# One tuned encoder kernel: the root of six of its eight RMS norms reaches the partitions by other ways

## The chip, the cores and the metric

The kernel runs on one core of a Trainium2 chip. The metric is the device time of one execution in microseconds (us). The core has a matrix engine (TensorE, PE in the rows; its weight loads are PEld), a vector engine (VectorE, DVE), a scalar engine (ScalarE, ACT), a general engine (GpSimd, POOL) and a queue of transfers that one more engine issues in order (SyncE, SP). Each engine takes its own instructions in program order and waits on semaphores for the others.

## The reference, cut to what matters

One layer of a hybrid encoder, applied to 1024 prompt tokens and 256 sample tokens with 1024 features, all in float32, then a last norm:

```python
def rmsnorm(x, w):
    xf = x.astype(jnp.float32)
    y = xf * lax.rsqrt(jnp.mean(xf * xf, -1, keepdims=True) + EPS)
    return (y * w.astype(jnp.float32)).astype(x.dtype)
```

The layer has three sublayers with residual adds. Each begins with this norm. The first is a mixing block (a gated DeltaNet, which is a chunked linear recurrence, beside a gated two-layer branch, gMLP), then cross-attention into 256 + 256 memory tokens, which are normalised too, then a SwiGLU feed-forward block. So a norm is needed of the tokens before the mixing block, before the attention, of the memory, before the feed-forward block, and at the end. For one token the sum of squares runs over the 1024 features, and its inverse root then scales all 1024 features of the token.

## The kernel before

**Tiling.** Activations lie feature-major: 1024 features are 8 tiles (KT = 8) of 128 partitions, and the tokens run along the free axis. There are three token blocks: 0 and 1 of 512 prompt tokens each, 2 of 256 sample tokens. Large products are float32 split in two rounded parts (hi and lo, or whi and wlo for weights), and three matmuls stand for one product. They come from helper lines L108 (`mm`), so L108 is nearly every matmul of the trace. `split` makes the parts: ACT writes hi (L125), DVE or POOL subtracts to get lo (L126).

**What sets the order.** The program is built by Python generators. PE's order is written out: the main stream of products runs, and side generators (a norm is one) `yield` a number of nanoseconds of PE work after which their next step is put in. `lag`, `lag2` and `pace` are such numbers. So a norm's products stand at a fixed place in PE's stream, ready or not. The other engines' instructions are ordered by a scheduler that sees dependencies and its own costs. SP's transfers are issued in its order, one behind another.

**A norm.** `Norm.add` squares tile after tile on ACT (L259) and sums them on DVE (L260) into `nacc`. `Norm.rest` sums over the partitions with narrow products into a bank, so that each token's sum lies on a partition; L280 makes the mean, and L231 to L235 on DVE find the inverse root by three Newton steps into the tile `nst`, 128 partitions x 4 (token number c * 128 + p on partition p, column c), or x 2 for block 2. The root must then come from "token on a partition" to "token on the free axis, the same in all partitions". Before, that is one float32 product for each 128 tokens: the column of roots, broadcast, as weights against the identity (`cst`), into a PSUM bank. In the trace they are the rows `bank<-cst,nst`: four products for 512 tokens, two for 256, and each product leaves two records. Then L298 on DVE scales each of the 8 tiles by weight and root (`nt<-mem,sm,bank` for the memory, `x<-x,sm,bank` for the others), and a sink passes it on: stores of the memory tiles (`md`), `split` of the feed-forward input, stores of the output (`yT`).

```python
pb = bank()
for c in range(nb):
    mm(pb[:, c * P : (c + 1) * P], y[:, c : c + 1].to_broadcast([P, P]), ident)
```

**The places.** Eight norms use this code. Two (the mixing block's) are not touched. The memory's norm runs around 90 to 105 us, while the in-projection of block 2 goes through PE; on DVE and ACT the gMLP's gelu groups run then (L497 to L500, the `gt` and `vg` tiles), then the layer norm's statistics (L519 to L525, `sums`), the DeltaNet's decay rates (L549 to L568, `ab`, `beta`, `wk`, `gm`), and the scaling of the gMLP's `vg` (L529). PE takes `gm` in the product `bank<-cst,gm` and `vg` in `bank<-sw,vg`. The feed-forward norms of blocks 0, 1, 2 stand at 1295, 1337 and 1355 us, in the attention's out-projection (`OutProj.run`; L1491 is its residual add out of PSUM) and the first products behind it. The final norms of blocks 1 and 0 are at 2093 and 2127 us (`last_norm`). There the sample block's feed-forward inputs (`graw`, L2333) are loaded by SP, split into `gs` (L126), and the down-projection's results are added by L2254.

## Time and profile before

Three runs took 2184.56, 2186.04 and 2183.62 us, median 2184.56. The profile is of one more execution.

| | us |
|---|---|
| median of the runs | 2184.56 |
| profiled execution, its own time | 2183.43 |
| profiled execution, first to last instruction (span) | 2181.6 |
| PE busy | 2168.0 (99 %) |
| DVE busy | 1356.4 (62 %) |
| ACT busy | 885.9 (41 %) |
| POOL busy | 592.4 (27 %) |
| mean granted clock of TensorE | 0.999 of full speed |

In a row of the timeline stand the start in us, the duration in us (of all the instructions that the row groups, with their count behind the x), engine, line, operation, output and inputs by tile name, shapes; in brackets the idle time of the engine ahead of it and who ended it. Matmuls overlap in the pipeline, so a matmul's price is the distance between the starts of two neighbours, not its duration.

### The profile page before, as it was taken

How to read it: one execution, taken by the hardware profiler on the slowest of the kernel's cores; microseconds unless marked ns; L12 is line 12 of the kernel's file. 1: busy time of each engine (PE TensorE's matmuls, PEld its weight loads, DVE VectorE, ACT ScalarE, POOL GpSimd, SP SyncE). 2: the span in 40 equal slices, each digit the busy share in tenths (PEclk: the TensorE clock that was granted, in tenths of full speed). 3: DMA queues.
4: the chain of work that ended last, by engine and by line, in shares of the span. 5: the costliest groups of instructions: out<-in, count | busy, mean ns of one | idle time of the engine just before them, and what ended most of it. 6: DMA issues, size and time to landing. Idle time of an engine off the chain costs nothing.

```text
span 2181.6 us, 31947 instructions
## 1 busy us (share of the span) xinstructions
PE 2168.0 (99%) x12184; PEld 1888.0 (87%) x12184; DVE 1356.4 (62%) x2615; ACT 885.9 (41%) x1651; POOL 592.4 (27%) x399
## 2 busy tenths in 40 slices
PE   9999999999999999999999999999999999999998
PEld 8988888888988888888988888888888888888888
DVE  7867688786874846677644556544434444478575
ACT  6533363544535553125544523332322323343454
POOL 2010100101001010052412432566666665200031
PEclk9999999999999999999999999999999999999999
DMA  5221323323244546631522421322222222493531
GB/s 195 92 93 57 109 63 96 82 66 95 75 122 121 171 133 228 204 128 58 175 73 111 156 97 64 104 87 83 83 78 81 83 97 91 149 347 119 205 112 59
DMA packets 194296, 253.04 MB, mean 116 GB/s; under 512 B 76932, under 2 KB 109268, under 8 KB 194142
## 3 DMA queue, kind: packets, MB, share of 16 engines
q1 hardware_dynamic: 177886, 227.14, 31.6%
q10 hardware_dynamic: 16256, 23.86, 3.0%
q8 instruction: 95, 1.56, 0.3%
q14 instruction: 59, 0.48, 0.1%
HBM read 178.02 MB, written 72.94 MB: 115 GB/s over the span
## 4 chain that ended last, share of the span: by engine, by line
PE 95%; DVE 2%; ACT 1%; DMA 1%; issue 0%; SPq 0%; POOL 0%; DVEq 0%; ACTq 0%; POOLq 0%
PE bank L108 94%; PE bank L121 1%; DMA braw<-gq 1%; DVE gb L832 0%; PE bank L398 0%; DVE aT L827 0%; DVE nt L298 0%; DVE nacc L260 0%; DMA uc<-usd 0%; DVE sw L1014 0%; POOL lo L126 0%; DVE wlo L126 0%; ACT junk L524 0%; ACT whi L125 0%; DVE bhl L126 0%
## 5 line engine op out<-in xcount | busy, mean ns | idle before, releaser
L108 PE MATMUL bank<-hi,whi 128*128 128x512 f32 (+1 forms) x1976 | 700.6, 355 | 0.0
L108 PE MATMUL bank<-lo,whi 128*128 128x512 f32 (+1 forms) x1976 | 687.0, 348 | 0.0
L108 PE MATMUL bank<-hi,wlo 128*128 128x512 f32 (+1 forms) x1976 | 686.6, 347 | 0.0
L108 PEld LDWEIGHTS bank<-hi,wlo 128*128 128x128 f32 x1976 | 373.6, 189 | 47.8
L108 PEld LDWEIGHTS bank<-hi,whi 128*128 128x128 f32 x1976 | 374.4, 189 | 45.1 <-issue 1.1
L108 PEld LDWEIGHTS bank<-lo,whi 128*128 128x128 f32 x1976 | 374.5, 190 | 43.3 <-issue 0.2
L126 POOL TENSOR_TENSOR wlo<-raw,whi 128x1024 fp32r<-128x1024 f32 x65 | 158.1, 2433 | 296.5 <-ACT whi L125 296.5
L125 ACT ACTIVATE whi<-raw 128x1024 fp32r<-128x1024 f32 (+1 forms) x136 | 137.0, 1009 | 249.1 <-PE bank L108 216.8
L126 DVE TENSOR_TENSOR wlo<-raw,whi 128x1024 fp32r<-128x1024 f32 (+1 forms) x71 | 80.8, 1141 | 74.7 <-ACT whi L125 74.4
L108 PE MATMUL bank<-bhl,whi 128*128 128x512 f32 x408 | 125.8, 390 | 0.0
L126 POOL TENSOR_TENSOR wlo<-x,whi 128x1024 fp32r<-128x1024 f32 x40 | 96.6, 2414 | 47.5 <-ACT whi L125 47.5
L2136 DVE TENSOR_TENSOR x<-x,bank 128x512 f32<-128x512 f32 x21 | 14.5, 689 | 124.4 <-ACT x L1931 124.4
L108 PEld LDWEIGHTS bank<-bhl,whi 128*128 128x128 f32 x408 | 76.5, 188 | 16.1
L710 DVE SCALAR_TENSOR_TENSOR acc<-craw,sm,acc 128x510 f32<-128x510 f32 (+1 forms) x96 | 73.2, 763 | 23.8 <-ACT acc L708 22.1
L1944 DVE SCALAR_TENSOR_TENSOR t<-t,x 128x512 f32<-128x512 f32 x42 | 63.9, 1521 | 28.7 <-ACT t L1943 28.7
L125 ACT ACTIVATE whi<-x 128x1024 fp32r<-128x1024 f32 (+1 forms) x48 | 49.2, 1025 | 77.5 <-PE bank L108 69.6
L108 PE MATMUL bank<-bhl,wlo 128*128 128x512 f32 x204 | 79.6, 390 | 0.2 <-DVE wlo L126 0.2
L1953 DVE SCALAR_TENSOR_TENSOR t<-bank,t 128x512 f32<-128x512 f32 (+1 forms) x44 | 24.5, 558 | 81.4 <-PE bank L108 81.4
L108 PE MATMUL bank<-bhl,ahl 128*128 128x512 f32 x312 | 75.0, 395 | 0.0
L1082 ACT ACTIVATE gs<-bank 128x512 f32<-128x512 f32 (+1 forms) x60 | 31.2, 520 | 101.2 <-PE bank L108 93.9
L1931 ACT ACTIVATE x<-bank 128x512 f32<-128x512 f32 x63 | 37.6, 597 | 82.0 <-PE bank L108 79.3
L108 PEld LDWEIGHTS bank<-bhl,ahl 128*128 128x128 f32 x312 | 58.7, 188 | 13.6
(420 smaller groups left out, 4462.6 us busy)
## 6 DMA issues: line engine op xcount, KB each, us to landing
raw<-in_w_gu SPq DMA_DIRECT2D x44, 512.0 KB, 3.3
braw<-gq SPq DMA_DIRECT2D x14, 1024.0 KB, 6.9
raw<-in_w_g SPq DMA_DIRECT2D x20, 512.0 KB, 3.3
gq<-t SPq DMA_DIRECT2D x33, 256.0 KB, 2.0
gtd<-gs ACTq DMA_DIRECT2D x32, 256.0 KB, 2.1
w<-in_w_dn SPq DMA_DIRECT2D x8, 1024.0 KB, 9.6
raw<-in_w_qkv SPq DMA_DIRECT2D x12, 512.0 KB, 3.4
gq<-r SPq DMA_DIRECT2D x22, 256.0 KB, 2.0
```

Of the source, the lines that this page charges most:

```text
L108: self.nc.tensor.matmul(out, l, r, start=start, stop=stop, skip_group_check=more)
L121: self.nc.tensor.transpose(out, x, ident)
L125: self.last_hi = self.nc.scalar.activation(hi, src, AF.Copy).ins
L126: (eng or self.nc.vector).tensor_tensor(out=lo, in0=src, in1=f32(hi), op=ALU.subtract)
L710: V.scalar_tensor_tensor(out=dst, in0=src, scalar=wj, in1=dst, op0=ALU.mult, op1=ALU.add)
L1082: S.activation(t, ps, AF.Tanh, scale=0.5)
L1931: S.activation(t, ps, AF.Copy)
L1944: V.scalar_tensor_tensor(out=t, in0=t, scalar=1.0, in1=src, op0=ALU.add, op1=ALU.mult)
L1953: V.scalar_tensor_tensor(out=out, in0=u, scalar=sign, in1=t, op0=ALU.mult, op1=ALU.mult)
L2136: V.tensor_tensor(out=c22, in0=c22, in1=pe, op=ALU.add)
```

## The change

The sums, the roots, the weights' scaling and the sinks stay. Three ways now bring the root to the partitions:

- The memory norm and the feed-forward norm of block 0 take the way over DRAM: SP writes `nst` (4 numbers, 16 bytes a partition) to `rows_d`, and SP reads the 512 numbers back into all 128 partitions of the norm's own accumulator `nacc`. No product is made. The scaling (L323 now) reads its root from SBUF, not from a bank, through a view that puts the token order right (`quad`).
- The feed-forward norms of blocks 1 and 2 and the final norms of blocks 1 and 0 are "spread": DVE rounds the root to its high part (L294, `nhi`), subtracts for the low part (L295), and multiplies the identity by each part, broadcast (L299, tile `nd`, 128x512 or 128x256; L293 rounds a column of ones). Then two products of the ones with `nd` as moving operand, as wide as the block and with rounded inputs, fill the bank. `nd` takes buffers of the tag `nsq`, from which the squares and, at the end, the `graw` tiles come too.
- The two norms of the mixing block are unchanged, as is the norm of block 2 at the end.

`lag2` grows from 2800 to 6500 for the memory (and ROW = 3500 ahead of it), and from 2800 to 7000 for block 0; for the others the place of the products stays (SPREAD is taken out of `lag2` and put back).

```diff
@@ -260,7 +260,7 @@
                 (eng or V).tensor_tensor(out=self.acc, in0=self.acc, in1=sq, op=ALU.add)
             self.k += 1
 
-        def rest(self, xk, wcol, sink, pace=1300, shared=(), lag=1500, ks=range(KT), inplace=False, ready=None, halves=1, lag2=2800, rooms=(), behind=None):
+        def rest(self, xk, wcol, sink, pace=1300, shared=(), lag=1500, ks=range(KT), inplace=False, ready=None, halves=1, lag2=2800, rooms=(), behind=None, row=None, spread=False):
 
             p, n = self.p, self.n
             nb = n // P
@@ -272,30 +272,55 @@
             for c in range(nb):
                 for t in parts:
                     mm(pc[:, c : c + 1], t[:, c * P : (c + 1) * P], one, t is parts[0], t is parts[-1])
-            y = p.tile([P, 4 if p is xp else 16], F32, tag="nst", name="nst", bufs=2)[:, :nb]
+            rest_ = p.tile([P, 4 if p is xp else 16], F32, tag="nst", name="nst", bufs=2)
+            y = rest_[:, :nb]
             ms, sc = pc[:, 4 : 4 + nb], pc[:, 8 : 8 + nb]
             with ExitStack() as st:
                 if behind is not None:
                     st.enter_context(tc.issue_after(behind()))
                 V.tensor_scalar(out=ms, in0=pc[:, :nb], scalar1=1.0 / D, scalar2=EPS, op0=ALU.mult, op1=ALU.add)
             K.root_end = rsqrt(y, ms, sc)
-            yield lag2
-            pb = bank()
-            for c in range(nb):
-                mm(pb[:, c * P : (c + 1) * P], y[:, c : c + 1].to_broadcast([P, P]), ident)
+            if row is not None:
+                SY.dma_start(row.rearrange("(p c) -> p c", c=nb), y)
+                yield ROW
+                SY.dma_start(self.acc, row.unsqueeze(0).to_broadcast([P, n]))
+                yield lag2
+                rb = pb = self.acc.rearrange("q (p c) -> q c p", c=nb)
+            elif spread:
+                yield lag2 - SPREAD
+                rounded = p.tile([P, 16], F32R, tag="nhi", name="nhi")
+                yhi, ylo = f32(rounded[:, 4 : 4 + nb]), rest_[:, 8 : 8 + nb]
+                V.tensor_copy(rounded[:, 0:1], one)
+                V.tensor_copy(rounded[:, 4 : 4 + nb], y)
+                V.tensor_tensor(out=ylo, in0=y, in1=yhi, op=ALU.subtract)
+                spreads = []
+                for part in (yhi, ylo):
+                    t = p.tile([P, 512], F32R, tag="nsq", name="nd", bufs=self.sq)[:, :n]
+                    V.tensor_tensor(out=quad(t), in0=ident.unsqueeze(1).to_broadcast([P, nb, P]), in1=part.unsqueeze(2).to_broadcast([P, nb, P]), op=ALU.mult)
+                    spreads.append(t)
+                yield SPREAD
+                pb = bank()[:, :n]
+                for t in spreads:
+                    mm(pb, rounded[:, 0:1].to_broadcast([P, P]), t, t is spreads[0], t is spreads[-1])
+            else:
+                yield lag2
+                pb = bank()[:, :n]
+                for c in range(nb):
+                    mm(pb[:, c * P : (c + 1) * P], y[:, c : c + 1].to_broadcast([P, P]), ident)
             while ready is not None and not ready():
                 yield 300
-            if shared:
+            like = (lambda x: x) if row is None else quad
+            if shared and row is None:
                 rb = self.acc
-                S.activation(rb, pb[:, :n], AF.Copy)
+                S.activation(rb, pb, AF.Copy)
             for k in ks:
                 if k in shared:
                     S.activation(xk(k), xk(k), AF.Copy, scale=sm[:, wcol + k : wcol + k + 1])
-                    G.tensor_tensor(out=xk(k), in0=xk(k), in1=rb, op=ALU.mult)
+                    G.tensor_tensor(out=like(xk(k)), in0=like(xk(k)), in1=rb, op=ALU.mult)
                     sink(k, xk(k))
                     continue
                 t = bank() if k in rooms else xk(k) if shared or inplace else p.tile([P, 512], F32, tag="nsq", name="nt", bufs=self.sq)[:, :n]
-                V.scalar_tensor_tensor(out=t, in0=xk(k), scalar=sm[:, wcol + k : wcol + k + 1], in1=pb[:, :n], op0=ALU.mult, op1=ALU.mult)
+                V.scalar_tensor_tensor(out=like(t), in0=like(xk(k)), scalar=sm[:, wcol + k : wcol + k + 1], in1=pb, op0=ALU.mult, op1=ALU.mult)
                 sink(k, t)
                 yield pace * n / 512
 
@@ -313,12 +338,12 @@
         rsqrt(y, ms, sc)
         yield lag2
 
-    def norm(p, xk, n, wcol, sink, pace=1300, step=700, lag=1500):
+    def norm(p, xk, n, wcol, sink, pace=1300, step=700, lag=1500, **more):
         nm = Norm(p, n)
         for k in range(KT):
             nm.add(xk(k))
             yield step
-        yield from nm.rest(xk, wcol, sink, pace, lag=lag)
+        yield from nm.rest(xk, wcol, sink, pace, lag=lag, **more)
 
     def to_h(h, b, mine=(1, 3, 5, 7)):
         return lambda k, t: split(h[b][0][:, k, :], h[b][1][:, k, :], t, V if k in mine else G)
@@ -460,6 +485,7 @@
     begin.close()
 
     done = set()
+    rows_d = dp.tile([2, 512], F32, name="rows_d")
 
     def other_norms():
         nm = Norm(xp, 512)
@@ -472,7 +498,7 @@
         done.add(1)
         mem = x_load(a["memT"], 0, 512, "mem")
         yield 6000
-        yield from norm(xp, lambda k: mem[:, k, :], 512, S_MEM, lambda k, t: SY.dma_start(md[k], t))
+        yield from norm(xp, lambda k: mem[:, k, :], 512, S_MEM, lambda k, t: SY.dma_start(md[k], t), lag2=6500, row=rows_d[0])
 
     norms = K.side(other_norms())
 
@@ -1523,7 +1549,7 @@
                 if sinks is None:
                     norm_b = nms[b].rest(xk, wcol, to_h(hs, b), 600)
                 else:
-                    norm_b = nms[b].rest(xk, wcol, sinks(b, hs), PACES[b], ks=range(KT) if b != 1 else SECOND_KS, inplace=True, lag2=LAGS2[b])
+                    norm_b = nms[b].rest(xk, wcol, sinks(b, hs), PACES[b], ks=range(KT) if b != 1 else SECOND_KS, inplace=True, lag2=LAGS2[b], row=rows_d[1] if b == 0 else None, spread=b > 0)
                 K.pending[id(hs), b] = K.side(norm_b)
             self.x = x
 
@@ -2293,7 +2319,7 @@
             (SY if k % 2 else S).dma_start(a["yT"][:, k, t0 : t0 + n], t)
 
         if b < 2:
-            K.side(nm.rest(lambda k: x2[b][:, k, :], S_FIN, sink, PACEF, SHARED[b], LAGF[b], lag2=LAGF2[b]))
+            K.side(nm.rest(lambda k: x2[b][:, k, :], S_FIN, sink, PACEF, SHARED[b], LAGF[b], lag2=LAGF2[b], spread=True))
             return
         pb = bank()
         ms, y = pb[:, :n], pb[:, n : 2 * n]
@@ -2418,9 +2444,10 @@
 MIX = 6500
 A1, A2, A3, A4 = 1200, 800, 2000, 600
 DEC, CONV = 1200, 600
-FIRST_W, PACES, LAGS2 = 9000, (600, 1300, 600), (2800, 9500, 9500)
+FIRST_W, PACES, LAGS2 = 9000, (600, 1300, 600), (7000, 9500, 9500)
 LAGX = (26000, 17000, 9000)
 FIRST_V = (1, 3, 5, 6, 7)
+ROW, SPREAD = 3500, 2500
 LAG0, LAGF, LAGF2, PACEF = 9700, (8000, 6000, 1500), (9000, 9000, 2800), 1000
 
 SHARED, EARLY_K = ((1, 4, 6), (1, 3, 5, 7)), (1, 3)
```

PE's order is the same but for these products: 4 fewer at the memory, 4 fewer at block 0, two in place of four at blocks 1 (feed-forward and final) and 0 (final), two in place of two at block 2. On the other engines rows move. Lines behind L280 are renumbered (L298 is L323 now, L1491 is L1517, L519 is L545, L555 to L568 are L581 to L594).

VectorE at the memory norm, before: the last four of eight scalings `nt` and what follows.

```order
L298 SCALAR_TENSOR_TENSOR nt<-mem,sm,bank 128x512
L500 SCALAR_TENSOR_TENSOR vg,sums<-gt,bank 128x248
L621 COPY ab<-bank 128x16
L298 SCALAR_TENSOR_TENSOR nt<-mem,sm,bank 128x512 x2
L498 SCALAR_TENSOR_TENSOR gt<-gt,bank 128x248
L298 SCALAR_TENSOR_TENSOR nt<-mem,sm,bank 128x512
L500 SCALAR_TENSOR_TENSOR vg,sums<-gt,bank 128x248
L621 COPY ab<-bank 128x16
L519 TENSOR_TENSOR sums<-sums 128x4
L550 TENSOR_TENSOR wk_1280<-ab,rows 128x80
```

The same place now, from a little further on; between L545 (L519 before) and these rows stand one more L323 and the four L575 (L549):

```order
L576 TENSOR_TENSOR wk_1263<-ab,rows 128x80
L546 TENSOR_SCALAR sums<-sums 128x4
L323 SCALAR_TENSOR_TENSOR nt<-mem,sm,nacc 128x512
L577 SCALAR_TENSOR_TENSOR wk_1263<-wk_1263 128x80
L547 TENSOR_SCALAR sums<-sums 128x4
L323 SCALAR_TENSOR_TENSOR nt<-mem,sm,nacc 128x512
L589 TENSOR_SCALAR wk_1263<-wk_1263 128x80
L581 TENSOR_SCALAR wk_1263<-wk_1263 128x80
L582 RECIPROCAL wk_1263<-wk_1263 128x80
L323 SCALAR_TENSOR_TENSOR nt<-mem,sm,nacc 128x512
L583 TENSOR_TENSOR wk_1263<-wk_1263 128x80
```

Before, all eight scalings stood ahead of L519 (`sums`). Now the first stands behind two more gelu groups, and four of the eight stand behind L545, between the small instructions on `wk` that make `gm`.

VectorE at the feed-forward norm of block 1, from the end of the root (L235) to the first scaling. Before:

```order
L235 SCALAR_TENSOR_TENSOR nst<-bank,nst 128x4
L1491 SCALAR_TENSOR_TENSOR x_12386<-bank,x_12386 128x256
L260 TENSOR_TENSOR nacc<-nacc,nsq 128x256
L1491 SCALAR_TENSOR_TENSOR x_12386<-bank,x_12386 128x256
L260 TENSOR_TENSOR nacc<-nacc,nsq 128x256
L1491 SCALAR_TENSOR_TENSOR x_12386<-bank,x_12386 128x256
L260 TENSOR_TENSOR nacc<-nacc,nsq 128x256
L298 SCALAR_TENSOR_TENSOR x_12385<-x_12385,sm,bank 128x512 x2
```

Now:

```order
L235 SCALAR_TENSOR_TENSOR nst<-bank,nst 128x4
L294 CAST nhi<-nst 128x4
L295 TENSOR_TENSOR nst<-nst,nhi 128x4
L1517 SCALAR_TENSOR_TENSOR x_12384<-bank,x_12384 128x256
L260 TENSOR_TENSOR nacc<-nacc,nsq 128x256
L1517 SCALAR_TENSOR_TENSOR x_12384<-bank,x_12384 128x256
L299 TENSOR_TENSOR nd<-cst,nhi 128x512
L260 TENSOR_TENSOR nacc<-nacc,nsq 128x256
L299 TENSOR_TENSOR nd<-cst,nst 128x512
L1517 SCALAR_TENSOR_TENSOR x_12384<-bank,x_12384 128x256
L260 TENSOR_TENSOR nacc<-nacc,nsq 128x256
L323 SCALAR_TENSOR_TENSOR x_12383<-x_12383,sm,bank 128x512 x2
```

L294, L295 and the two L299 have come in; the second L299 stands behind two more sums L260, whose places relative to L1517 have changed by one.

VectorE at the feed-forward norm of block 2, before:

```order
L1896 TENSOR_TENSOR x_12384<-x_12384,x_12385 128x1024
L235 SCALAR_TENSOR_TENSOR nst<-bank,nst 128x2
L1953 SCALAR_TENSOR_TENSOR t<-bank,t 128x512
L126 TENSOR_TENSOR lo_12699<-x_12384,hi_12698 128x1024
L298 SCALAR_TENSOR_TENSOR x_12386<-x_12386,sm,bank 128x256 x4
L126 TENSOR_TENSOR lo_12701<-x_12386,hi_12700 128x256
```

Now:

```order
L1922 TENSOR_TENSOR x_12382<-x_12382,x_12383 128x1024
L235 SCALAR_TENSOR_TENSOR nst<-bank,nst 128x2
L1979 SCALAR_TENSOR_TENSOR t<-bank,t 128x512
L294 CAST nhi<-nst 128x2
L126 TENSOR_TENSOR lo_12697<-x_12382,hi_12696 128x1024
L295 TENSOR_TENSOR nst<-nst,nhi 128x2
L299 TENSOR_TENSOR nd<-cst,nhi 128x256
L299 TENSOR_TENSOR nd<-cst,nst 128x256
L126 TENSOR_TENSOR lo_12697<-x_12382,hi_12696 128x1024
L323 SCALAR_TENSOR_TENSOR x_12384<-x_12384,sm,bank 128x256 x4
```

A `lo` split of 128x1024 stands between the end of the root and L295, as it stood between L235 and L298 before.

On SP at the end, 14 loads `graw` stood ahead of block 1's four stores `yT`, then 2, then 6; now 9 stand ahead, then 5, then 8. On DVE, three `gs` splits stood between block 1's scalings and the first L2254 of block 0; now two stand there, one more ahead of the scalings, and two behind the first L2280 (L2254 before), ahead of the other three. POOL's and ACT's own orders hold no new instruction.

## The prediction

> **What bounds the kernel now.** I read the page first, its busy times and the chain of work that ended last:
>
> ```profile
> PE 2168.0 (99%) x12184; PEld 1888.0 (87%) x12184; DVE 1356.4 (62%) x2615; ACT 885.9 (41%) x1651; POOL 592.4 (27%) x399
> PE 95%; DVE 2%; ACT 1%; DMA 1%; issue 0%; SPq 0%; POOL 0%; DVEq 0%; ACTq 0%; POOLq 0%
> ```
>
> PE sets the end: nearly all of the chain is its work, and the other engines hold it up for a few per cent. So a product taken away is worth its place in PE's stream, unless PE then waits for something else; and each delay of an operand of PE's next product costs its full length. Next the root's products, all of them in the view by tile, and one norm (feed-forward, block 0) and the smaller one (block 2) in PE's timeline:
>
> ```profile
> L108 PE MATMUL bank<-cst,nst x60: 270/275/376, 30.1 to 2127.8; 128*128 128x128 f32 x60
> ...
> 1295.00 1.05 PE L108 MATMUL bank<-cst,nst 128*128 128x128 f32 x8
> 1295.80 0.48 PE L108 MATMUL bank<-hi,whi 128*128 128x512 f32 x1
> 1296.12 0.39 PE L108 MATMUL bank<-lo,whi 128*128 128x512 f32 x1
> 1296.35 0.39 PE L108 MATMUL bank<-hi,wlo 128*128 128x512 f32 x1
> ...
> 1355.29 0.61 PE L108 MATMUL bank<-cst,nst 128*128 128x128 f32 x4
> 1355.65 0.48 PE L108 MATMUL bank<-hi,whi 128*128 128x512 f32 x1
> ```
>
> 60 records are 30 products in eight norms. Four products hold PE from 1295.00 to 1295.80, and the next product takes 0.32 to the one behind it where its like takes 0.23: 0.89 us for four, and 0.36 + 0.09 = 0.45 for two (the same 0.09 taken). That is all the change can take from PE: a rounded 512-wide product costs 0.23, and a 256-wide one, an estimate from that, half, 0.12. So the bound on the gain is 0.89 at the memory, 0.89 at block 0, 0.89 - 0.45 = 0.44 at each of three 512-wide spread norms, 0.2 at block 2: **3.3 us, 0.15 %**. Less than 0.2 % (4.4 us) is about what a measurement of this kernel can tell from no change.
>
> **What the new work costs on VectorE.** What comes in reads its tensors from SBUF alone: the scalings L323 of two norms (x and nacc), L295, L299. Such instructions behave in their own way beside POOL:
>
> ```profile
> 92.67 0.17 DVE L234 TENSOR_TENSOR bank<-bank,nst 128x4 f32<-128x4 f32 x1
> 109.54 2.36 DVE L234 TENSOR_TENSOR sums<-sums 128x4 f32<-128x4 f32 x1
> ...
> 109.46 2.43 POOL L126 TENSOR_TENSOR wlo<-raw,whi 128x1024 fp32r<-128x1024 f32 x1 [35.38 <-ACT whi L125]
> 115.02 2.59 POOL L126 TENSOR_TENSOR wlo<-raw,whi 128x1024 fp32r<-128x1024 f32 x1 [3.14 <-ACT whi L125]
> ```
>
> The same four-element product takes 0.17 alone and 2.36 when both inputs lie in SBUF and POOL's split began just ahead: it ended at 111.90, with the split (111.89). So such an instruction waits for the end of POOL's running one.
>
> **Memory norm.** PE loses 0.89. The rows around it:
>
> ```profile
> 94.91 0.16 DVE L235 SCALAR_TENSOR_TENSOR nst<-bank,nst 128x4 f32<-128x4 f32 x1
> 100.44 0.41 DVE L498 SCALAR_TENSOR_TENSOR gt<-gt,bank 128x248 f32<-128x248 f32 x1 [0.41 <-ACT gt L497]
> 101.85 1.39 DVE L298 SCALAR_TENSOR_TENSOR nt<-mem,sm,bank 128x512 f32<-128x512 f32 x2
> 104.78 0.16 DVE L519 TENSOR_TENSOR sums<-sums 128x4 f32<-128x4 f32 x1
> 113.19 0.44 DVE L568 SCALAR_TENSOR_TENSOR gm<-wk,rows 128x32 f32<-128x32 f32 x4
> 114.81 4.00 DVE L529 TENSOR_SCALAR vg<-vg,sums 128x512 f32<-128x512 f32 x4
> ...
> 76.98 1.91 DVE L529 TENSOR_SCALAR vg<-vg,sums 128x512 f32<-128x512 f32 x4
> ...
> 115.45 0.63 PE L108 MATMUL bank<-cst,gm 128*40 128x128 f32 x4
> 117.88 1.47 PE L108 MATMUL bank<-sw,vg 128*128 128x128 f32 x8
> 119.11 0.47 PE L108 MATMUL bank<-hi,whi 128*128 128x512 f32 x1
> ...
> md<-nt SPq DMA_DIRECT2D x8, 256.0 KB, 2.0
> xsd<-gb SPq DMA_DIRECT2D x40, 32.0 KB, 1.7
> ```
>
> The row's way: the root is there at 95.07. The trace has no transfer of 16 bytes a partition and no read-back of a row; the nearest are the small store `xsd<-gb`, 1.7 us from issue to landing, and 2.0 for `md<-nt`. I take 1.7 + 2.0 and some 0.5 of issue: landed at about 99.3. By the order the first L323 now stands behind the gelu step of 100.44, which comes 0.89 earlier, at 99.55 to 99.96: the row is there, barely. One scaling takes about 0.66 (101.85, 1.39 for two that overlap a little). Whether the stepped view `quad` slows them is not in the trace; I take no change, and a doubling (0.66 for each of the four late ones, 2.6) as the upper bound.
>
> Between L519 and the `gm` of L568 VectorE is nearly never idle (8.4 us, 2.2 of them the stall above), and four scalings, 2.64 us, now stand inside. With all ahead 0.89 earlier, `gm` would start at 113.19 - 0.89 + 2.64 = 114.94. POOL's second split then runs from 114.13 to 116.72, and `gm` has both inputs in SBUF: it starts at 116.72, ends at 117.16. PE had it at 115.45: **+1.7**. Behind it the `vg` scalings no longer meet the split (1.91 us, not 4.00), and the eight records of `sw,vg`, which took 1.23 to the next product because the last `vg` came at 118.81, go through in about 0.87: -0.36. Sum of the stage, the 0.89 in it: **+1.4**; at best -0.89 (if `gm` slips in before the split), at worst +2.6 (all four scalings on the path and the saving lost elsewhere in the stage).
>
> The Trainium skill (DMA: Bandwidth & Descriptors, Specifications) has a rule against this way: transfers below 512 bytes are read, changed and written back by the DMA engine. It gives no time for it; were the write twice as long, an estimate from the row above, the rows would come at 101, and the stage would stay as it is.
>
> **Block 0.** 0.89 goes. The row is written and read behind a store, and its scalings feed products much later:
>
> ```profile
> 1297.39 2.73 DVE L298 SCALAR_TENSOR_TENSOR x<-x,sm,bank 128x512 f32<-128x512 f32 x4 [0.75 <-DMA x2d<-x]
> ...
> 1341.84 0.40 PE L108 MATMUL bank<-hi,whi 128*128 128x512 f32 x1
> ```
>
> The scalings wait for that store already, and the first 512-wide product of the feed-forward block stands 44 us behind: the way over DRAM is hidden, up to some 30 us. **-0.89**. Without that cover it would cost the trip, 4.2 us.
>
> **Feed-forward, block 1.** The place with the dearest new wait:
>
> ```profile
> 1330.83 0.16 DVE L235 SCALAR_TENSOR_TENSOR nst<-bank,nst 128x4 f32<-128x4 f32 x1
> 1333.31 0.41 DVE L1491 SCALAR_TENSOR_TENSOR x<-bank,x 128x256 f32<-128x256 f32 x1
> 1336.36 1.26 DVE L260 TENSOR_TENSOR nacc<-nacc,nsq 128x256 f32<-128x256 f32 x1 [0.54 <-ACT nsq L259]
> ...
> 1330.70 2.41 POOL L126 TENSOR_TENSOR wlo<-raw,whi 128x1024 fp32r<-128x1024 f32 x1 [0.47 <-ACT whi L125]
> 1333.19 5.59 POOL L1876 TENSOR_TENSOR raw<-raw 128x512 f32<-128x512 f32 x4
> ...
> 1336.63 1.05 PE L108 MATMUL bank<-cst,nst 128*128 128x128 f32 x8
> ```
>
> The add L1491, with an input in a bank, takes 0.41 in the midst of POOL's work: its kind doesn't wait. POOL is busy from 1330.70 to 1338.78: a split to 1333.11, then four of 1.40, ending at 1334.59, 1335.98, 1337.38, 1338.78. The sum L260 of 1336.36 ends 0.24 behind such an end already (1337.62). Now step by step in the new order: root done 1330.99 (L294, four elements, some 0.1 behind it); L295 waits to 1333.11 and ends at 1333.3; the add L1517 to 1333.65; L260 waits to 1334.59, ends 1334.85; L1517 to 1335.2; the first L299 waits to 1335.98 and ends half a microsecond later, 1336.5; L260 waits to 1337.38, ends 1337.62; the second L299 waits to 1338.78, ends 1339.3. PE wanted both at 1336.63: 2.7 late, less 0.44: **+2.25**. Without a lock the same list needs 2.8 us, is done at 1333.8, and the stage gives -0.44; if each of the five waits a whole POOL instruction, it ends at 1340.25: +3.2.
>
> **Feed-forward, block 2.** POOL rests here, VectorE's queue is what counts:
>
> ```profile
> 1354.44 1.22 DVE L126 TENSOR_TENSOR lo<-x,hi 128x1024 fp32r<-128x1024 f32 x1
> ```
>
> L295 and the two L299 stand behind that split: 1355.6, then 0.1, 0.35 and 0.42 (the 128x256 add L1491 above took 0.41, its successor less behind it): 1356.45. With two products of 0.12 PE goes on at 1356.6, not 1355.65: **+0.95** (-0.2 with the work in time, +1.3 if the split takes its slowest).
>
> **Final norms.** PE loses 2 x 0.44. VectorE's new work at the last norm (L295 and two L299, some 1.4 us) lies in idle time: in the view of waits its `wlo` splits wait for ACT there, six times, 3.6 us in all.
>
> ```profile
> DVE wlo L126 <- ACT whi L125: 3.6, 6, 0.7
> ```
>
> But `nd` takes buffers from `graw`, and five of its loads move behind four stores that wait for the scalings:
>
> ```profile
> 2096.17 4.55 SPq L2293 DMA_DIRECT2D yT<-x  x4
> 2100.94 0.82 SPq L2333 DMA_DIRECT2D graw<-gsd  x2
> ...
> 2103.79 0.69 DVE L2254 SCALAR_TENSOR_TENSOR x<-bank,x 128x512 f32<-128x512 f32 x1 [0.47 <-PE bank L108]
> 2106.51 0.69 DVE L2254 SCALAR_TENSOR_TENSOR x<-bank,x 128x512 f32<-128x512 f32 x1 [0.67 <-PE bank L108]
> 2107.46 4.71 DVE L126 TENSOR_TENSOR wlo<-w,whi 128x512 fp32r<-128x512 f32 x4 [0.25 <-ACT whi L125]
> ```
>
> Issued from 2100.9 at 0.41 apart and landing some 2 us later, they come at 2103 to 2105; the `gs` splits that need them stand ahead of and between the adds L2254 on VectorE, whose second then comes near 2106.2, 2.4 late. VectorE's idle time to 2107.46 is 0.47 + 0.67 + 0.25 = 1.4, so 1.0 is left for PE: -0.88 + 1.0 = **+0.1** (-0.9 to +1.5).
>
> **Sum:** 1.4 - 0.89 + 2.25 + 0.95 + 0.1 = +3.8. The profiled execution took 2183.43, 1.1 below the median, and would take 2187.2; on the median of 2184.56 that is **2188.4 us**, +0.17 %.
>
> **The rivals.**
> - *The vector work fits.* If the waits at POOL fall out otherwise (POOL's work moves with VectorE's, `gm` slips ahead of the split) all stages give what PE saves: -3.3, 2181.3 us. For it: PE's places are kept, and `lag2` leaves 5 us at block 1. Against it: L260 already ends with POOL's instructions. Chance 0.15.
> - *VectorE's locks set the end* (slower for certain): at block 1 every two-input instruction waits a whole POOL instruction, +3.2, and the memory stage pays +2.6: 3.8 + 0.95 + 1.2 = +6.0, 2190.6 us. It decides once `gm` starts later than 116.72 and L299 meets POOL's last. For it: the row of 2.36; against it: L260 at 1336.36 met only the rest of one. Chance 0.22.
> - *The memory row comes late.* VectorE stands at the first L323, and the gelu groups, `sums` and `gm` behind it. `gm` has 116.72 - 114.94 = 1.8 us of room, so from 101.7 on (a trip of 6.7 us) each microsecond costs one; 8 us cost 1.3: 2189.7 us. Chance 0.06.
> - That the change does not do what it says is excluded by the order, which shows the products gone.
>
> **How the numbers follow.** Forecast 0.52 (own range 2186 to 2190.5), the rivals 0.15, 0.22, 0.06, something else 0.05. The lines lie at 2180.2 and 2188.9. Faster: a fifth of the first rival and a little of the rest, 0.05. Slower: the second and third rival and 0.3 of the forecast's case, 0.44. Same: what is left, 0.51. The range begins just under the first rival's time and ends 0.9 above the second's; with the upper bound of the stepped view (2.6) on a forecast that is otherwise right it still holds 2191.0: 2181.2 to 2191.5. Left out are half of the first rival, some of the second and of the rest: 0.2.
>
> **What would show it.** Right: `gm` on VectorE starting with the end of POOL's split, and PE idle ahead of `bank<-cst,gm`; the second L299 of block 1 ending with a POOL instruction, after 1338; PE idle 0.9 ahead of block 2's `bank<-nd,nhi`; no idle at block 0. Wrong: L299 at 0.7 us each inside POOL's four, or `gm` on time (then 2181 to 2185), or VectorE idle ahead of the first `nt` for the row (then over 2189).

## The result, and the profile after

The changed kernel takes 2201.57 us (median of six runs, 2200.51 to 2201.80). The kernel before, timed beside it, takes 2184.55 (2183.62 to 2186.04). The ratio is 1.0078, with a 95% interval of 1.0068 to 1.0088: **17 us slower**, where the forecast was 3.8 slower and the range ended 6.9 above the median before. The direction was right, and so were most of the places; the size was not. Two executions at a lower granted clock (2374.76 us at 0.849, with the memory norm as before, and 3072.45 us at 0.654, with the rows alone) are not in the medians given below.

The page of the changed kernel, busy times and chain of work:

```profile
PE 2171.5 (99%) x12148; PEld 1887.5 (86%) x12148; DVE 1373.3 (62%) x2635; ACT 886.4 (40%) x1651; POOL 592.2 (27%) x399
PE 87%; DVE 8%; DMA 2%; ACT 1%; issue 1%; POOL 0%; SPq 0%; DVEq 0%; ACTq 0%; POOLq 0%
```

PE has 36 records less and is busy 3.5 us *more*, and its share of the chain fell from 95% to 87%, with VectorE at 8%. So two things happened: PE waits for VectorE, and some of PE's work takes longer than it did.

**Where the 17 us lie.** PE's order is the same in both kernels but for the root's products, so each remaining product can be found in both traces, and the difference of its two start times tells how far the changed kernel has fallen behind there. That difference, at products named by their time in the trace of before:

| stretch of before | fallen behind | what lies in it | forecast |
|---|---|---|---|
| 90 to 125 | +7.1 | memory norm | +1.4 |
| 125 to 1290 | +0.8 | nothing changed | 0 |
| 1290 to 1310 | -1.0 | feed-forward norm, block 0 | -0.89 |
| 1310 to 1334 | +0.4 | block 0's last scalings, on VectorE | 0 |
| 1334 to 1353 | +3.9 | feed-forward norm, block 1 | +2.25 |
| 1353 to 1365 | +1.0 | feed-forward norm, block 2 | +0.95 |
| 1365 to 1392 | +0.6 | behind it | 0 |
| 1392 to 1900 | +1.6 | feed-forward products of block 2 | 0 |
| 1900 to 2090 | +0.1 | | 0 |
| 2090 to 2135 | +2.6 | final norms (-0.4, +3.5, -0.4) | +0.1 |
| sum | +17.1 | the spans: 2198.7 - 2181.6 | +3.8 |

**The memory norm.** SP's queue of the changed kernel (start, time, line, tiles, transfers; a time of several is from the first to the last of them):

```profile
95.04 0.32 SPq L284 DMA_DIRECT2D rows_d<-nst  x1
97.50 0.32 SPq L286 DMA_DIRECT2D nacc<-rows_d  x1
102.21 12.50 SPq L501 DMA_DIRECT2D md<-nt  x8
114.80 6.17 SPq L139 DMA_DIRECT2D raw<-in_w_qkv  x2
```

The read of the row can be issued when the write has landed, 2.46 us behind it. VectorE and POOL there (a wait and what ended it stand in brackets):

```profile
101.03 1.15 DVE L323 SCALAR_TENSOR_TENSOR nt<-mem,sm,nacc 128x512 f32<-128x512 f32 x1 [1.13 <-DMA nacc<-rows_d]
...
111.34 3.02 DVE L323 SCALAR_TENSOR_TENSOR nt<-mem,sm,nacc 128x512 f32<-128x512 f32 x1
...
118.36 2.35 DVE L590 SCALAR_TENSOR_TENSOR wk<-wk 128x80 f32<-128x80 f32 x1
120.74 0.45 DVE L594 SCALAR_TENSOR_TENSOR gm<-wk,rows 128x32 f32<-128x32 f32 x4
...
111.03 2.39 POOL L126 TENSOR_TENSOR wlo<-raw,whi 128x1024 fp32r<-128x1024 f32 x1 [37.00 <-ACT whi L125]
118.26 2.35 POOL L126 TENSOR_TENSOR wlo<-raw,whi 128x1024 fp32r<-128x1024 f32 x1 [4.84 <-DMA raw<-in_w_qkv]
```

The first scaling waits 1.13 for the row, and takes 1.15, not the 0.74 of its like before. The last one, at 111.34, starts inside POOL's first split (111.03 to 113.42) and ends behind it; `wk` at 118.36 does the same with the second. That second split itself starts 3.24 later than before (118.26 against 115.02), because its `raw` stood on SP behind the eight stores `md`, the last of which waits for the last scaling. Those rows of SP in the kernel before:

```profile
97.18 7.58 SPq L475 DMA_DIRECT2D md<-nt  x8
111.91 6.06 SPq L139 DMA_DIRECT2D raw<-in_w_qkv  x2
```

So `gm` starts at 120.74, 7.55 behind its time before. PE there, and the granted clock (in the row of the window: time, PE and its products, PEld, DVE, ACT, POOL, clock, DMA share, GB/s):

```profile
113.47 0.39 PE L108 MATMUL bank<-hi,wlo 128*128 128x256 f32 x1 [0.47 <-POOL wlo L126]
...
121.06 1.07 PE L108 MATMUL bank<-cst,gm 128*40 128x128 f32 x4 [5.79 <-DVE gm L594]
...
122.66 0.42 PE L108 MATMUL bank<-hi,wlo 128*128 128x256 f32 x1
122.87 0.42 PE L108 MATMUL bank<-hi,whi 128*128 128x256 f32 x1
...
122.00:123.00 1.00, 1.00 (x5) 0.94 (x5) 1.00 (x3) 0.00 (x0) 0.00 (x0) 0.50 0.85 340
```

PE idles 5.79 us, and then `bank<-cst,gm` takes 1.07 instead of 0.63 and a 256-wide product 0.21 from start to start, where the prediction's estimate for it was 0.12: by the clock's record the granted clock is 0.50 from 118.31, while PE still waits, to 125.14. From 121.06 on some 1.8 us are lost that way, **a term that the forecast didn't have**.

**Feed-forward, block 1.** VectorE, POOL and PE from the end of the root:

```profile
1338.21 2.12 DVE L294 CAST nhi<-nst 128x4 fp32r<-128x4 f32 x1
...
1342.24 1.45 DVE L299 TENSOR_TENSOR nd<-cst,nhi 128x512 fp32r<-128x512 f32 x1
...
1345.03 1.75 DVE L299 TENSOR_TENSOR nd<-cst,nst 128x512 fp32r<-128x512 f32 x1
...
1337.90 2.41 POOL L126 TENSOR_TENSOR wlo<-raw,whi 128x1024 fp32r<-128x1024 f32 x1 [0.48 <-ACT whi L125]
1340.38 5.84 POOL L1902 TENSOR_TENSOR raw<-raw 128x512 f32<-128x512 f32 x4
...
1346.83 0.60 PE L108 MATMUL bank<-nd,nhi 128*128 128x512 f32 x1 [2.58 <-DVE nd L299]
...
1348.00:1349.00 1.00, 1.00 (x7) 1.00 (x6) 1.00 (x3) 0.23 (x1) 0.00 (x0) 0.50 0.00 0
```

The second `nd` ends at 1346.78, half a microsecond behind POOL's last `raw` (1346.22). PE waits 2.58 for it, and again runs at a clock of 0.50 afterwards, from 1347.11 to 1350.52.

**Block 2**, as foreseen:

```profile
1365.52 0.16 DVE L294 CAST nhi<-nst 128x2 fp32r<-128x2 f32 x1
...
1367.36 0.62 PE L108 MATMUL bank<-nd,nhi 128*128 128x256 f32 x2 [0.82 <-DVE nd L299]
```

**From 1392 to 1900** no wait has come in, yet PE falls behind steadily. The view by tile shows one group of products there, of before and of after (minimum, median and maximum in ns):

```profile
L108 PE MATMUL bank<-t4h,wlo x84: 389/389/389, 1390.2 to 1889.5; 128*128 128x512 f32 x84
```

```profile
L108 PE MATMUL bank<-t4h,wlo x84: 393/394/395, 1402.9 to 1903.8; 128*128 128x512 f32 x84
```

The products whose moving operand is `t4h` or `t4l` stand in 21 groups of twelve (252 records). From the start of one to the start of the next, the first five of a group take 228 to 236 ns before and the other seven 226 or 227; after, all twelve take 232 to 240. Summed over the 252 that is 1.3 us, 5 ns each; the remaining 0.4 lies in the products between the groups.

**The final norms.** SP, ACT, VectorE and PE:

```profile
2110.22 4.54 SPq L2319 DMA_DIRECT2D yT<-x  x4
2114.80 2.56 SPq L2359 DMA_DIRECT2D graw<-gsd  x5
...
2118.05 1.97 ACT L125 ACTIVATE gs<-graw 128x512 fp32r<-128x512 f32 x3 [3.23 <-DMA graw<-gsd]
2119.33 0.68 DVE L2280 SCALAR_TENSOR_TENSOR x<-bank,x 128x512 f32<-128x512 f32 x1
...
2121.87 0.50 PE L108 MATMUL bank<-gs,whi 128*128 128x256 f32 x2 [1.01 <-DVE x L2280]
2125.97 0.39 PE L108 MATMUL bank<-gs,wlo 128*128 128x256 f32 x1 [0.61 <-DVE wlo L126]
2128.27 0.39 PE L108 MATMUL bank<-gs,wlo 128*128 128x256 f32 x1 [0.60 <-DVE wlo L126]
```

Five loads of `graw` stand behind the stores `yT`; ACT waits 3.23 for the first of them, the add L2280 stands behind the `gs` split that waits for ACT, and PE waits three times. In the kernel before PE has no wait at these products.

### The profile page after: what moved, and what is told of

It reads as the page before. It is cut to its first block, busy times and chain, and to the rows that moved or that the text cites. A ratio compares the mean times of both kernels' runs of the same rounds, so it can differ in the third digit from the quotient of the medians.

```text
span 2198.7 us, 31892 instructions
## 1 busy us (share of the span) xinstructions
PE 2171.5 (99%) x12148; PEld 1887.5 (86%) x12148; DVE 1373.3 (62%) x2635; ACT 886.4 (40%) x1651; POOL 592.2 (27%) x399
## 4 chain that ended last, share of the span: by engine, by line
PE 87%; DVE 8%; DMA 2%; ACT 1%; issue 1%; POOL 0%; SPq 0%; DVEq 0%; ACTq 0%; POOLq 0%
PE bank L108 86%; PE bank L121 1%; DVE wlo L126 1%; DVE x L323 1%; DMA braw<-gq 1%; DVE nt L323 0%; DVE W L885 0%; DVE nacc L260 0%; DVE W L888 0%; DVE lo L126 0%; ACT whi L125 0%; DMA rows_d<-nst 0%; DMA nacc<-rows_d 0%; DVE gb L858 0%; POOL x L319 0%
```

## The experiments

The theory after the result: (a) at the memory the row comes late, its stepped view makes the scalings slow, and SP's stores hold the next load; (b) each long wait of PE is followed by a stretch at half clock, which costs again; (c) at block 1 VectorE stands behind POOL; (d) the drift from 1392 to 1900 comes from where `t4h` lies in SBUF; (e) at the end it is the place of the `graw` loads. A negative difference of a stage below is a gain against the kernel before. Diffs are against the changed kernel, the last one against the kernel before.

**Memory norm as before.**

```diff
-...norm(xp, ..., lag2=6500, row=rows_d[0])
+...norm(xp, ...)
```

> The changed kernel, with the memory norm as it was before (four products, scalings from the bank); all else changed. Theory of stages: each stage costs by itself what PE's stream shows when the two profiles are laid side by side (memory +7.1, block 0 -0.7, block 1 +4.1, block 2 +1.1, final norms +2.7, and a drift of 2.3 between 1384 and 1907 us). Then this takes 2201.5 - 7.1 = 2194.4 us, and PE is not idle ahead of bank<-cst,gm. Rival, one wait hides the next: PE that comes earlier out of the memory stage waits for loads or for POOL later; then the time stays above 2197.

Measured: 2194.4 us, ratio 1.0044 (1.0031 to 1.0058); `bank<-cst,gm` at 115.96 with no wait ahead, and the stage costs 0.0. The memory norm carries some 7 of the 17 us.

**Scalings of the memory held back** behind a copy that comes after `gm` (the copy of `gr`, L602), with the row's way as it is:

```diff
-...norm(xp, ..., lag2=6500, row=rows_d[0])
+...norm(xp, ..., lag2=36000, row=rows_d[0], after=lambda: K.gr_end)
...
+with tc.issue_after(after()):
     V.scalar_tensor_tensor(out=like(t), ...)
```

> The changed kernel; the memory norm still goes over DRAM, but its eight scalings are held on VectorE behind the copy of gr (119 us in the trace of before), that is behind gm and vg. Theory, the place: what costs is that the row's wait and the scalings stand ahead of gm; behind it nobody waits for them, and the stage gives what PE saves, -0.9 in place of +7.1: 2193.5 us. Rival, the way: a read-back that takes 6 us and scalings of 1.1 us cost wherever they stand, since VectorE's gelu and mx work stands among them; then at least 3.4 us (eight times 0.42) stay of the 7.1, and the time is above 2196.

Measured: 2193.22 us, ratio 1.0042 (1.0027 to 1.0057). PE's product with `gm`, and the scalings in the view by tile:

```profile
114.39 0.63 PE L108 MATMUL bank<-cst,gm 128*40 128x128 f32 x4
...
L326 DVE SCALAR_TENSOR_TENSOR nt<-mem,sm,nacc x8: 1119/1129/1166, 118.5 to 130.4; 128x512 f32<-128x512 f32 x8
```

The scalings are as slow as ever, but nothing that PE needs stands behind them: no wait, full clock, and the stage gives -0.96. So the row over DRAM is worth its 0.89 where nobody waits for it, and what cost 7.1 was the place of the scalings on VectorE and SP.

**Unit step, small pieces.** The row is written so that its tokens lie in order in DRAM (pieces of 4 bytes, not 16), and read with step one:

```diff
-SY.dma_start(row.rearrange("(p c) -> p c", c=nb), y)
+SY.dma_start(row.rearrange("(c p) -> p c", c=nb), y)
...
-rb = pb = self.acc.rearrange("q (p c) -> q c p", c=nb)
+rb = pb = self.acc
```

> The changed kernel; the rows are written to DRAM in token order (4 bytes apart from each partition, 512 pieces, in place of 16 bytes), so that the scalings L323 read their root with a step of 4 bytes, not of 16. Theory, the step: an L323 takes 0.74 again, not 1.15, gm comes 8 x 0.42 = 3.4 us sooner, and the time is about 2198 us. Rival, the place of the operand: two tensors from SBUF are what makes it slow, L323 stays at 1.15, 2201.5 us or, with a slower write, more.

Measured: 2211.81 us, ratio 1.0130 (1.0115 to 1.0145), 14 us above what was expected:

```profile
94.92 0.37 SPq L284 DMA_DIRECT2D rows_d<-nst  x1
105.12 0.32 SPq L286 DMA_DIRECT2D nacc<-rows_d  x1
...
108.88 0.75 DVE L323 SCALAR_TENSOR_TENSOR nt<-mem,sm,nacc 128x512 f32<-128x512 f32 x1 [9.10 <-DMA nacc<-rows_d]
```

The scaling takes 0.75, so the step of 16 bytes is what makes it 1.15: that part of the theory holds. But the write's 512 pieces of 4 bytes need 10.2 us to the next issue, where 128 pieces of 16 bytes needed 2.46, and VectorE waits 9.10. The expectation had taken the trip as unchanged. Not all of the loss is the memory's: that stage costs 12.9 here, and the stretch from 1310 to 1334, where the changed kernel lost 0.4, costs 7.8. At block 0 the write needs 10.8 us too, VectorE waits 7.57 for that row at 1321, and behind its scalings stands the sum of block 1, for which PE waits 4.34 up to 1341; the clock is 0.50 from 1338.69 to 1348.93.

**Unit step, large pieces.** PE turns the roots (a transposition of `nst`), VectorE copies the four rows into SBUF, and the write has four pieces of 512 bytes:

```diff
-SY.dma_start(row.rearrange("(p c) -> p c", c=nb), y)
+pt = bank()
+tr(pt[:nb, :P], y, ident)
+yt = self.acc[:nb, :P]
+V.tensor_copy(yt, pt[:nb, :P])
+SY.dma_start(row.rearrange("(c p) -> c p", c=nb), yt)
...
-rb = pb = self.acc.rearrange("q (p c) -> q c p", c=nb)
+rb = pb = self.acc
```

> The changed kernel; the roots are first turned by one transposition on TensorE (128x4 to 4x128, 3.3 us of PE work behind the sums) and copied to SBUF, so that the row goes out as 4 pieces of 512 bytes in token order, and L323 (here a few lines further on) reads its root with a step of 4 bytes. Five of the eight memory scalings stand behind sums, not four. Theory, the step and the write apart: write about 2 us, scalings 0.75 in place of 1.15, gm some 3 us sooner than in the changed kernel (8 x 0.42, less one scaling more behind sums), the memory stage +4 in place of +7: about 2198.5 us. Rival, the pieces do not matter and the row stays late as with 512 pieces: 2205 us or more.

Measured: 2197.44 us, ratio 1.0059 (1.0044 to 1.0075):

```profile
96.07 0.32 SPq L289 DMA_DIRECT2D rows_d<-nacc  x1
97.29 0.35 SPq L291 DMA_DIRECT2D nacc<-rows_d  x1
...
104.23 0.74 DVE L328 SCALAR_TENSOR_TENSOR nt<-mem,sm,nacc 128x512 f32<-128x512 f32 x1
...
118.19 0.63 PE L108 MATMUL bank<-cst,gm 128*40 128x128 f32 x4 [3.60 <-DVE gm L599]
```

1.2 us for the write and 0.74 for a scaling. The stage costs 4.0 against 7.1: with both the step and most of the write's time gone, VectorE still gives `gm` 3.60 us too late. Five scalings stand between `sums` and `gm`, and VectorE meets both of POOL's splits ahead of `gm` (2.34 us at 109.69 and 2.34 at 114.93), where before it met one (2.36 at 109.54).

**Feed-forward, blocks 1 and 2, as before** (block 0 keeps its row):

```diff
-..., row=rows_d[1] if b == 0 else None, spread=b > 0)
+..., row=rows_d[1] if b == 0 else None)
```

> The changed kernel, with the feed-forward norms of blocks 1 and 2 as before (block 0 keeps its row). Theory of stages: 2201.5 - 4.1 - 1.1 = 2196.3 us, no idle PE at 1344, no stretch at half the clock there; the drift of 2.3 us behind them stays. Rival: the drift comes from these two norms (it begins behind them); then it goes too, 2194.0 us.

Measured: 2192.83 us, ratio 1.0041 (1.0026 to 1.0056). From 1334 to 1900 the kernel falls behind by 0.00 us, where the changed kernel lost 7.1: the drift goes with the two norms, the case for which the expectation named 2194.0, 1.2 above what was measured.

**A longer `nhi`,** which puts everything behind it in SBUF on another address:

```diff
-rounded = p.tile([P, 16], F32R, tag="nhi", name="nhi")
+rounded = p.tile([P, 64], F32R, tag="nhi", name="nhi")
```

> The changed kernel with one number changed: the small tile nhi (16 numbers, 64 bytes a partition) is 64 numbers (256 bytes) long. In the compiled programs' memory maps the tiles t4h and t4l of the feed-forward block begin at byte 177920 and 186112 of a partition before (multiples of 256) and 64 bytes lower in the changed kernel; in the changed kernel all twelve products of each t4h group take 233 ns, before only the first five do. With the long tile they begin at multiples of 256 again. Theory, the address: the drift of 2.3 us goes, 2199.2 us, and the products go back to 227 ns. Rival: the drift comes from something else that these norms bring (timing of the splits against PE): 2201.5 us, 233 ns.

Measured: 2199.55 us, ratio 1.0072 (1.0057 to 1.0087). The products, in the view by tile, and the byte at which the tile starts in a partition, by the program's allocation: 177920 before, 64 less after (177856, 64 beyond a multiple of 128), 256 less here (177664, a multiple of 128 again).

```profile
L108 PE MATMUL bank<-t4h,wlo x84: 389/389/389, 1402.3 to 1901.6; 128*128 128x512 f32 x84
```

The distance is 12.06 at 1392 and 12.06 at 1900: the drift is gone, with the norms still spread. So it is the address of something in SBUF, which the 64 bytes of `nhi` moved. That it is the moving operand's own is the nearest reading, since three quarters of the loss lie in its products; the other tiles behind `nhi` moved with it and were not tested apart. In the time only part of it is seen: by the traces 1.8 us went at 1900 to 1912, where PE waits for weights, and 4.6 at the final norms instead of 3.5.

**`nd` made by ACT** in the feed-forward norms, 128 columns at a time:

```diff
+for c in range(nb if inplace else 0):
+    S.activation(t[:, c*P:(c+1)*P], ident, AF.Copy, scale=part[:, c:c+1])
+if not inplace:
     V.tensor_tensor(out=quad(t), ...)
```

> The changed kernel; in the feed-forward norms of blocks 1 and 2 the tiles nd are made on ACT (128 columns at a time, scaled by the root's part), not on VectorE; L294 and L295 stay on VectorE. Theory, the lock: what makes block 1 late is that L299 and the sums between them wait for POOL's instructions; ACT waits for none, both nd are there before PE asks (1343.8), PE has no idle time and no half clock there, and block 1 gives -0.4 in place of +4.1: 2197.0 us. Block 2 stays at +1. Rival, the chain's length: nd is late because L294 and L295 end late and the work behind them is long; ACT's eight instructions come no sooner: 2200 us or more.

Measured: 2198.45 us, ratio 1.0068 (1.0052 to 1.0085), 1.5 above the expectation. Block 1:

```profile
1338.28 2.11 DVE L294 CAST nhi<-nst 128x4 fp32r<-128x4 f32 x1
...
1343.96 1.26 ACT L300 ACTIVATE nd<-cst,nst 128x128 fp32r<-128x128 f32 x4
...
1345.27 0.49 PE L108 MATMUL bank<-nd,nhi 128*128 128x512 f32 x1 [0.67 <-ACT nd L300]
```

The stretch from 1334 to 1353 costs 1.0 instead of 3.9; the clock stays at 1.00. ACT isn't held by POOL's four instructions, VectorE was. Yet `nd` still came 0.67 late, where no wait had been expected. The cast L294 still stands 2.11 behind POOL's split. What the time didn't give back went at 1900 to 1912 (1.4 by the trace).

**Final norms as before.**

```diff
-...lag2=LAGF2[b], spread=True))
+...lag2=LAGF2[b]))
```

> The changed kernel, with the two final norms as before. Theory of stages, the loads graw moved behind the stores: they move back, and the end gives 2.7 us back: 2198.8 us, with fourteen graw loads ahead of the first yT on SP. Rival: the end is late because all before it is, and the products saved there (0.9 us) are lost: about 2202.4 us.

Measured: 2198.58 us, ratio 1.0068 (1.0053 to 1.0083). From 2090 to the end the distance doesn't move (16.53 to 16.52).

**Only the last norm spread** (block 0; block 1's final norm as before):

```diff
-...lag2=LAGF2[b], spread=True))
+...lag2=LAGF2[b], spread=b == 0))
```

> The changed kernel, with the final norm of block 1 as before and that of block 0 still spread. On SP fourteen graw loads stand ahead of the first yT again. Theory, block 1's two nd tiles push the loads: the end gives back 2.9 us and keeps 0.3 to 0.4 saved at block 0: 2198.3 us. Rival: block 0's spread is part of the loss (nd on VectorE among the wlo splits): above 2199.5.

Measured: 2198.15 us, ratio 1.0067 (1.0053 to 1.0080). SP there:

```profile
2090.54 17.71 SPq L2359 DMA_DIRECT2D graw<-gsd  x14
2111.16 4.55 SPq L2319 DMA_DIRECT2D yT<-x  x4
```

Fourteen `graw` loads stand ahead of the stores again, PE has no wait from 2100 to 2126, and the last norm keeps its -0.43. So the +3.5 belongs to block 1's final norm: its two `nd` take the buffers that five `graw` loads had.

**The rows alone, held back** (both rows, the memory's scalings late, no norm spread: the edits of the second, the fifth and the eighth experiment together).

> Only the two rows over DRAM, the memory's scalings held behind the copy of gr; the feed-forward norms of blocks 1 and 2 and the final norms as before. Theory of stages: memory -0.9, block 0 -0.7 to -0.9, nothing else: 1.6 to 1.8 us below the kernel before (2181.7 on its median of 2183.4). Rival: something that all kernels with this code share (the tile rows_d, the longer lag2) costs too; then no faster than before.

Measured: 2182.68 us beside 2183.95, ratio 0.9993 (0.9984 to 1.0003). By the trace 1.3 us are saved up to 1900, and 1.0 of it is given back by 1912. The place, in this kernel and in the one before:

```profile
1906.60 0.50 PE L108 MATMUL bank<-bhl,wlo 128*128 128x512 f32 x1 [0.52 <-DVE wlo L126]
```

```profile
1906.84 0.50 PE L108 MATMUL bank<-bhl,wlo 128*128 128x512 f32 x1 [0.18 <-DVE wlo L126]
```

PE waits longer here for the weights of the down-projection, but this wait is 0.3 of the 1.0. That the weights set the time at that place is not shown: in the traces the loss there differs from run to run (from -0.3 to +1.8 against the kernel before), and the next kernel, which comes there earliest, loses 0.2.

**The same with the last norm spread:**

```diff
-...lag2=LAGF2[b]))
+...lag2=LAGF2[b], spread=b == 0))
```

> The two rows, the memory's scalings behind gr, and the final norm of block 0 spread; the rest as before: every part of the change that was free where it stands. Theory of stages: -0.9 - 0.8 - 0.4 = 2.1 us of PE work saved. By the two rows alone, 1.4 us were saved by the middle of PE's stream and some was given back at 1901 to 1907 us, where PE waits for loads of weights that do not come sooner. So 2182.0 on a median before of 2183.9: faster, but by about 0.1 %, at the edge of what can be told. Rival: the saved products are swallowed by the wait for weights altogether, no difference.

Measured: 2182.07 us (11 runs, 2181.58 to 2183.13) beside 2183.74 (15 runs), ratio 0.9992 (0.9983 to 1.0001). By the trace it is 2.2 ahead at the end. The interval reaches past 1, so this is the best of the variants, but not shown to be faster: 1.7 us is less than a measurement here can tell.

**Waits alone.** In the kernel *before*, the root's products are put in earlier than the root is ready (block 0 by 2.8 us of PE's work, block 1 by 6.7), so that PE waits there and nothing else is changed:

```diff
-FIRST_W, PACES, LAGS2 = 9000, (600, 1300, 600), (2800, 9500, 9500)
+FIRST_W, PACES, LAGS2 = 9000, (600, 1300, 600), (0, 2800, 9500)
```

> The kernel before, with the root's products of the feed-forward norms put sooner in PE's stream (lag2 0 in place of 2800 at block 0, 2800 in place of 9500 at block 1), so that PE waits there for the root by some 2 us each. Nothing else changes but the places. It asks from which length of idleness the half clock begins: the changed kernel shows it behind 5.8 and 2.6 us, and not behind 1.0. Theory, the threshold lies below 2 us: a half clock for 3 to 4 us behind both, about +2 (wait) + 1.7 each, 7 us in all. Rival, it lies between 2 and 2.6: waits only, +4 us, clock 1.00 throughout.

Measured: 2198.2 us in one execution, 14.5 above the kernel before beside it, twice what the higher expectation said. There were four waits, not two:

```profile
1294.70 1.16 PE L108 MATMUL bank<-cst,nst 128*128 128x128 f32 x8 [2.64 <-DVE nst L235]
1335.82 1.16 PE L108 MATMUL bank<-cst,nst 128*128 128x128 f32 x8 [1.78 <-DVE nst L235]
1356.43 0.58 PE L108 MATMUL bank<-cst,nacc 128*128 128x1 f32 x4 [3.34 <-DVE nacc L260]
1370.31 0.68 PE L108 MATMUL bank<-cst,nst 128*128 128x128 f32 x4 [1.36 <-DVE nst L235]
...
1335.85:1337.00 1.15, 1.15 (x10) 1.15 (x11) 0.00 (x0) 0.00 (x0) 0.00 (x0) 1.00 0.00 0
1338.00:1340.00 2.00, 2.00 (x12) 2.00 (x11) 1.30 (x1) 0.67 (x2) 1.56 (x1) 0.50 0.00 0
```

The last two, for block 2's sum and its root, had not been foreseen. Behind each of the first three the clock is 0.50 for 3.41 us, and each time PE first starts again at full clock and is slowed 1.2 to 1.5 us later; behind the 1.36 it stays at 1.00. So a wait of 1.78 already brings the half clock, without any vector work or transfer of the changed kernel beside it, and (b) holds: the four waits add up to 9.1 us, three stretches of 3.41 us at half the clock cost about 1.7 each, 5.1, and the sum, 14.2, is nearly the whole of the 14.5.

The clock's record shows one thing more. Its changes lie on a grid of 3.413 us: in the changed kernel the record begins at 5.67 us, and the half clock 33 and 393 such steps later, at 118.31 and 1347.11; here it begins at 5.97, and the half clock 378, 390 and 396 steps later. In these two kernels the half clock fills just those steps that follow one with 1.78 us or more of idle time. So what a wait costs depends on where it falls on the grid: the 5.79 brought two steps, 6.83 us, and PE worked through 4.1 of them.

## Why the prediction was right and wrong, point by point

**Right.** The bound on what PE can gain: block 0 gave -1.0 for -0.89, and each final norm -0.43 for -0.44. Block 0's way over DRAM is hidden, though not by the "some 30 us" of room that the prediction gave it: where the row took some 14 us (unit step, small pieces) that place cost 7.8. Block 2's wait was 0.82 and its cost 1.0 for 0.95, by just the rows named. At block 1 it is POOL that VectorE waits for, the second L299 follows the end of POOL's last `raw`, and PE waits 2.58 where 2.7 was worked out. At the memory `gm` does start with the end of POOL's second split, and PE waits ahead of `bank<-cst,gm`.

**Wrong, memory norm (+1.4, measured +7.1).** Four steps of that sum failed.

- *The row's way* was taken as 1.7 + 2.0 + 0.5 = 4.2 us, from stores and loads of other shapes. It took 2.46 from the write's issue to the read's and 3.5 from there to the scaling, 6.0: VectorE waits 1.13. That rival, "the memory row comes late", was right on the wait, and had too much room in its price.
- *The stepped view* ("I take no change, and a doubling as the upper bound"). Each scaling takes 1.15, not 0.74, on all eight: 3.3 us. The upper bound had counted the four late ones only, though the four early ones are on VectorE's path as well once the first waits for the row. The Trainium skill (SBUF — State Buffer, Door 1: The DMA port swizzle) says that accesses which cross to a new 16-byte line pay, and that four float32 values fit in one. The root's view, alone of the three, steps by just 16 bytes, and the two runs with unit step agree: 0.74 and 0.75.
- *SP behind VectorE.* The prediction placed POOL's second split at 114.13. The stores `md` wait for the scalings, the load `raw` stands behind them on SP, and the split began at 118.26. `gm` was set by that end, 120.61, as worked out, but 3.9 us later than the 116.72 worked out.
- *PE's clock.* A wait was priced at its length. It was 5.79 us, and some 1.8 us were lost behind it at a clock of 0.50.

The sum by measured terms: waits of 5.79 and 0.47, 1.8 for the clock, less 0.89: 7.2, against 7.1 between the traces.

**Wrong, block 1 (+2.25, measured +3.9).** The wait had the right size, but the half clock behind it, some 1.7 us (3.41 at half speed), was not in the sum. One step of the working was off without moving its end: L294 was given 0.1, and took 2.12. At block 2, where POOL rests, it takes 0.16. It has one SBUF input only, and the prediction had said of such instructions that they don't wait (its example had its other input in a bank). The Trainium skill (SBUF — State Buffer, Who interferes with whom) lists copies and casts among those that can take the port which VectorE shares with GpSimd, and the trace agrees.

**Wrong, the final norms (+0.1, measured +2.6).** The five `graw` loads were named, and the two adds L2254 looked at. What was mis-sized is VectorE's room: 1.4 us of its idle time was taken to absorb 2.4 us of delay. But that idle time lies in pieces ahead of other instructions; ACT waits 3.23 for `graw`, and then three waits of PE, 1.01, 0.61 and 0.60, come in one after another, where the kernel before had none. In starts they move the products by 1.2, 0.8 and 0.8; the rest of the +3.5 is some 0.1 us more at each of several products right behind them. The range given for this term, -0.9 to +1.5, didn't hold it.

**Not in the prediction at all:** the 1.6 us from 1392 to 1900, by an address in SBUF, most likely that of `t4h` and `t4l`. No rival asked what a new tile does to the addresses of those behind it.

**Open.** The 0.8 us between 125 and 1290 and the 0.6 between 1365 and 1392: the former differs from run to run, in one run with the memory as before it is 1.5; the latter is there in each run with blocks 1 and 2 spread by VectorE and in none without. How much idle time within a step of the grid brings the half clock is not settled either: at the very end of three of the kernels a step with 1.9 us brought none, and in the run with small pieces one slow step came behind a step without idle time.

**The rivals.** "The vector work fits" was wrong everywhere but at block 0. "VectorE's locks set the end" was the nearest (+6.0), and the locks were there; what set the size lies in none of them. All prices were taken as if PE's wait ended when its operand came.

## What to carry to other kernels

Price a wait of the matrix engine with what follows it: here each of the waits of 1.78 to 3.60 us that stood alone brought 3.41 us at half clock, so up to 1.7 us went on top; the 5.79 brought twice that, part of it while PE still waited. Before work is moved into a vector engine's queue, follow its stores in the queue of transfers too: a store that waits for a late result holds the load behind it, and with it an engine that had nothing to do with the change. And when a small transfer is to replace a product, look at its layout at both ends: pieces too small cost in the write, and a step in the read costs on each use.

## What was not expected of the hardware

- **Half clock after short waits.** Behind waits of 3.60, 3.34, 2.64, 2.58 and 1.78 us the granted clock was 0.50 for 3.41 us, with the 5.79 for 6.83; behind 1.36, 1.01, 0.82 and 0.67 us it stayed at 1.00. Its changes lie on a grid of 3.413 us that begins at another time in each run. The Trainium skill (TensorE: Matmul & The Clock Gate, What's actually happening) gives an idle window of some 3.4 us for it, free-running. The length of a slow step and the grid agree; a wait of 1.78, half a window, was already enough, so the measurement goes further than the page.
- **Steps of 16 bytes on VectorE:** 1.15 us for 512 elements against 0.74 with unit step.
- **Pieces of a write to DRAM:** 2 KB took 1.2 us in 4 pieces of 512 bytes, 2.46 (memory) and 4.19 (block 0) in 128 of 16 bytes, and 10.2 and 10.8 in 512 of 4 bytes, from its issue to the issue of the read that waits for it.
- **An address in SBUF:** with the moving operand 64 bytes beyond a multiple of 128 most of its 512-wide products took 233 ns, not 227, from start to start; with 64 numbers in `nhi` in place of 16, the operand at a multiple of 128 again, they took 227.
- **A cast of four elements** from SBUF to SBUF, one input, waits for a running POOL instruction: 2.12 us against 0.16.
